# One layer of an RWKV-7/GLA backbone: the MLP's first product in seven block products for eight, and three passes over the tokens for two

## Chip, cores and metric

The kernel runs on one core of a Trainium2 chip. The time is device microseconds (us) of one execution of the whole program, from its first to its last instruction and what lies around them; the figure compared is the median of several runs.

## The reference, cut

One layer is computed for 256 prompt tokens and 2048 sample tokens, 2304 in all, with 1024 channels and an MLP width of 4096, in fp32. The change lies in the last four lines.

```python
def _block(x, mod, shift, states, p):
    sh1, sc1, gt1, sh2, sc2, gt2 = jnp.split(mod, N_MOD, axis=-1)
    h = _rmsnorm(x, p['norm1_g']) * (1.0 + sc1) + sh1
    o, new_states = _mixer(h, shift, ..., p)      # RWKV-7 and GLA heads, both directions
    x = x + gt1 * o
    h = _rmsnorm(x, p['norm2_g']) * (1.0 + sc2) + sh2
    f = jnp.square(jax.nn.relu(h @ p['mlp_w1'])) @ p['mlp_w2']
    x = x + gt2 * f
    return x, new_states                          # then y = _rmsnorm(x, final_norm_g)
```

The gate `gt2` (a row of 1024 numbers) is one for the prompt tokens and another for the sample tokens.

## The kernel before

Three stages follow each other: projections (`proj`), the two recurrences (`mixers`), and the `Tail`, which holds everything that is changed. The tail works on 18 units of 128 tokens. Their places in the token order are the list `UNITS`; units 9 and 10 are the prompt.

Numbers are kept at fp32 accuracy on TensorE (PE) by splitting each operand in two: `split` makes `hi`, a copy cast to fp32r on ScalarE (ACT), and `lo`, the rest, on VectorE (DVE). `mm3` then runs three matmuls (hi hi, hi lo, lo hi) into one bank of PSUM. There are 8 such banks.

- `unit(u)` normalises the mixers' outputs, multiplies by the output weights `wo` (48 matmuls of 512 columns), adds the residual, sends the result to DRAM (`d.x2`, "d_x" in the rows), norms again and transposes. The result, h2, is channels by tokens. Units 0 to 8 send it to DRAM (`d.h2`, "d_h" in the rows, 8 writes of 64 KB each). Units 9 to 17 split six of its eight row blocks straight into the SBUF tiles `h2h` and `h2l`; two row blocks go through DRAM, since their place is taken until then by `mh`, the split operand of the output product.
- `mlp(u0)` does 9 units, 1152 tokens, in 16 rounds. Round `gi` covers 256 of the 4096 middle channels. For each half of it a 512 KB piece of the first weights is loaded into `w1r` and split, and multiplied with three chunks of 384 tokens (8 x 3 matmuls of 384 columns each). Relu, square and split give `f`. Then each unit's second product (2 x 2 x 3 matmuls of 512 columns) is added to its accumulator `acc` by DVE. After round 13 (`PRE`) the accumulators are multiplied by the gate and the residual is added; in the last two rounds each product is multiplied by the gate as it is added. Round 15 ends with the final norm and the store.
- `reload` brings h2 back from DRAM between the two passes, `mlp(9)` and `mlp(0)`, 24 loads of 192 KB, each followed by a split.

All of the tail's instructions are recorded by `Plan`, which follows who reads and writes which part of a tile, gives each instruction an assumed cost, and issues them by list scheduling: of the instructions that could start, the one with the longest path behind it goes first. So the order on each engine isn't the order of the code. Every recorded instruction has line 534 in the profile, and the names of tiles tell them apart: "woh" and "wol" are the hi and lo parts of what lies over the output weights (first weights, second weights, f), "rr" is the buffer of relu and square. All DMAs are issued by SyncE (SP).

Of the kernel before, what the change touches and what calls it, by code (L numbers as in the profile page):

```python
# [185 lines left out]
BK_TAIL = [2, {"ps_t": 3, "ps_h": 1, "ps_m": 3, "ps_1": 3, "ps_2": 2}]  # L186
# [87 lines left out]
class Plan:  # L274
# [50 lines left out]
    def add(self, eng, method, args, kw):  # L325

        i = len(self.ops)
        if method == "matmul" and not kw["start"] and (args[1].dtype != F32R or len(self.ops[-1][1]) < 3):
            i -= 1
# [1211 lines left out]
MR = 2  # L1541
# [11 lines left out]
class Tail:  # L1553

    def __init__(self, g, es):
# [14 lines left out]
        self.rings = {
            "yo": acc[0:2], "gbs": [x[:, 0:1536] for x in acc[2:4]], "xt": [x[:, 1536:2048] for x in acc[2:4]],
            "x": [acc[4], xa, xb], "raw": [w1r, w2r, xa, xb], "m": halves(gf), "hf": halves(hf),
            "mh": [[w[:, 7 - i, 0:1024].rearrange("p (k n) -> p k n", k=8) for w in self.h] for i in range(MR)],
            "w1r": [w1r], "w2r": [w2r], "x2": [xa], "t": halves(xb), "r": [r[:, 0:384], r[:, 384:768]],
            "w1": [[wo[0][x][:, 1024 * i:1024 * i + 1024].rearrange("p (k n) -> p k n", k=8) for x in range(2)] for i in range(2)],
            "w2": [[wo[0][x][:, 2048 + 1024 * i:3072 + 1024 * i] for x in range(2)] for i in range(2)]
            + [[wo[1][x][:, 2304:3328] for x in range(2)]],
            "f": [[wo[1][x][:, 1152 * i:1152 * i + 1152] for x in range(2)] for i in range(2)],  # L1580
        }
        self.turn = dict.fromkeys(self.rings, 0)
        self.junk = r.bitcast(mybir.dt.bfloat16)[:, 0:1024]
# [30 lines left out]
    def unit(self, u):  # L1614
# [69 lines left out]
        for i in range(2):  # L1684
# [9 lines left out]
            k0 = 4 * i  # L1694
            k1 = k0 + 4 if u == 17 else min(k0 + 4, 8 - MR) if u >= 9 else k0
            if k1 > k0:
                cs = slice(128 * (u - 9), 128 * (u - 9) + 128)
                split(g, self.h[0][:, k0:k1, cs], self.h[1][:, k0:k1, cs], hf[:, 0:k1 - k0])
            for k in range(k1, k0 + 4):
                nc.sync.dma_start(out=d.h2[128 * k:128 * k + 128, us], in_=hf[:, k - k0])  # L1700

    def reload(self, k, u0, n):
        g = self.g
        raw = self.next("hf")[:, 0:128 * n]
        g.nc.sync.dma_start(out=raw, in_=g.d.h2[128 * k:128 * k + 128, 128 * u0:128 * (u0 + n)])
        cs = slice(128 * (u0 % 9), 128 * (u0 % 9 + n))
        split(g, self.h[0][:, k, cs], self.h[1][:, k, cs], raw)
# [133 lines left out]
```

## Time and profile before

| | us |
|---|---|
| median of 3 runs (lowest to highest) | 3704.69 (3702.34 to 3711.63) |
| the profiled execution | 3709.88 |
| its span, first to last instruction | 3708.2 |
| TensorE busy | 3504.4 (95%) |
| VectorE busy | 2249.8 (61%) |
| ScalarE busy | 1871.6 (50%) |
| GpSimd busy | 200.7 (5%) |

The projections and mixers fill the span up to about 1820 us, the units run to about 2090, the first MLP pass to about 2880 and the second to about 3690. Busy times are sums of single durations on one engine; engines work at the same time, so an engine's idle time costs something only where another waits for it. Matmuls overlap in PE's pipeline; the distance from one start to the next is the rate.

### The profile page before, as it was taken

What the parts mean: (1) busy time and instruction counts of PE and PEld (TensorE: products, weight loads), DVE (VectorE), ACT (ScalarE), POOL (GpSimd) and SP (SyncE); (2) the same over time, 40 slices, a digit from 0 to 9 for tenths busy, and PEclk for the clock granted to TensorE, in tenths of its full rate; (3) what the DMA queues carried; (4) which work ended last, traced back from release to release, by engine and by line L of the source; (5) the groups of instructions that cost most, each with busy time, mean ns of one, the idle gap of its engine ahead of it and who ended that gap; (6) DMA issues with size and microseconds to landing.
All of it is one profiled execution on the core that took longest, in us unless ns stands there. A gap on an engine that the chain in (4) does not pass through costs nothing.

```text
span 3708.2 us, 74382 instructions
## 1 busy us (share of the span) xinstructions
PE 3504.4 (95%) x28927; PEld 3104.1 (84%) x28927; DVE 2249.8 (61%) x4991; ACT 1871.6 (50%) x4264; POOL 200.7 (5%) x500
## 2 busy tenths in 40 slices
PE   6999999999999779999699999999999999999998
PEld 4989888977888668888587899999999899999997
DVE  2665778756888778788487534334447734444357
ACT  5566857775568567788567622222223422222222
POOL 1111002200011210100000000000000000000000
PEclk8999999999999889899799999999999999999999
DMA  5356335532245655565688411111114311111122
GB/s 170 110 152 172 103 84 167 145 107 56 62 129 160 181 159 168 154 193 164 168 250 248 146 40 46 35 40 46 46 43 136 130 34 46 46 46 40 46 70 101
DMA packets 504207, 411.47 MB, mean 111 GB/s; under 512 B 87761, under 2 KB 458926, under 8 KB 503854
## 3 DMA queue, kind: packets, MB, share of 16 engines
q1 hardware_dynamic: 503854, 406.71, 37.6%
q8 instruction: 228, 3.74, 0.4%
q14 instruction: 125, 1.02, 0.1%
HBM read 287.03 MB, written 119.55 MB: 110 GB/s over the span
## 4 chain that ended last, share of the span: by engine, by line
PE 46%; DMA 2%; DVE 1%; ACT 1%; issue 0%; DVEq 0%; SPq 0%; ACTq 0%
PE ps L534 46%; DVE acc L534 1%; DMA hf<-d_h 0%; ACT hf L534 0%; DMA xb<-in_w_out_dram 0%; DVE xb L534 0%; DMA xa<-in_x_sample_dram 0%; DVE h2l L534 0%; DMA d_h<-hf 0%; DMA xb<-in_x_sample_dram 0%; DMA acc<-in_x_prompt_dram 0%; DMA xa<-in_x_prompt_dram 0%; ACT xb L534 0%; ACT h2h L534 0%; DVE gf L534 0%
## 5 line engine op out<-in xcount | busy, mean ns | idle before, releaser
L534 DVE TENSOR_TENSOR acc<-acc,ps 128x512 f32<-128x512 f32 x468 | 319.8, 688 | 504.0 <-PE ps L534 503.5
L534 PE MATMUL ps<-hh,w_hi 128*128 128x384 f32 (+3 forms) x1736 | 594.2, 342 | 5.2 <-ACT w_hi L534 3.9
L534 PE MATMUL ps<-hh,w_lo 128*128 128x384 f32 (+3 forms) x1736 | 548.7, 316 | 0.9 <-DVE w_lo L534 0.9
L534 PE MATMUL ps<-hl,w_hi 128*128 128x384 f32 (+3 forms) x1736 | 549.0, 316 | 0.0
L534 ACT ACTIVATE rr<-ps 128x384 f32<-128x384 f32 x192 | 94.4, 492 | 869.2 <-PE ps L534 861.5
L534 PE MATMUL ps<-h2l,woh 128*128 128x384 f32 x1536 | 516.4, 336 | 0.6 <-DVE h2l L534 0.4
L534 PE MATMUL ps<-h2h,woh 128*128 128x384 f32 x1536 | 513.9, 335 | 0.9 <-ACT h2h L534 0.9
L534 PE MATMUL ps<-h2h,wol 128*128 128x384 f32 x1536 | 514.1, 335 | 0.0
L534 PE MATMUL ps<-woh,wol 128*128 128x512 f32 x1152 | 456.2, 396 | 0.0
L534 PE MATMUL ps<-wol,woh 128*128 128x512 f32 x1152 | 454.0, 394 | 0.0
L534 PEld LDWEIGHTS ps<-hh,w_hi 128*128 128x128 f32 (+1 forms) x1736 | 328.4, 189 | 39.1 <-issue 10.3
L534 PEld LDWEIGHTS ps<-hl,w_hi 128*128 128x128 f32 (+1 forms) x1736 | 329.0, 190 | 2.9 <-DVE hl L534 0.4
L534 PEld LDWEIGHTS ps<-hh,w_lo 128*128 128x128 f32 (+1 forms) x1736 | 327.9, 189 | 3.4 <-DVE w_lo L534 1.7
L534 PEld LDWEIGHTS ps<-h2l,woh 128*128 128x128 f32 x1536 | 288.3, 188 | 23.3 <-DVE h2l L534 1.6
L534 PEld LDWEIGHTS ps<-h2h,woh 128*128 128x128 f32 x1536 | 288.4, 188 | 21.2 <-ACT h2h L534 1.6
L534 PE MATMUL ps<-woh,woh 128*128 128x512 f32 x774 | 301.1, 389 | 0.5 <-ACT woh L534 0.5
L534 PEld LDWEIGHTS ps<-h2h,wol 128*128 128x128 f32 x1536 | 288.3, 188 | 0.0
L534 DVE TENSOR_TENSOR wol<-rr,woh 128x384 fp32r<-128x384 f32 x192 | 103.7, 554 | 267.4 <-ACT woh L534 267.4
L534 PEld LDWEIGHTS ps<-woh,wol 128*128 128x128 f32 x1152 | 215.9, 187 | 46.7 <-DVE wol L534 0.9
L534 PEld LDWEIGHTS ps<-wol,woh 128*128 128x128 f32 x1152 | 215.9, 187 | 31.2
L534 ACT CAST woh<-rr 128x384 fp32r<-128x384 f32 x192 | 95.7, 515 | 201.4 <-PE ps L534 198.4
L534 PEld LDWEIGHTS ps<-woh,woh 128*128 128x128 f32 x774 | 145.4, 188 | 21.5 <-ACT woh L534 0.8
(296 smaller groups left out, 6735.7 us busy)
## 6 DMA issues: line engine op xcount, KB each, us to landing
w_raw<-in_w_in_dram SPq DMA_DIRECT2D x72, 512.0 KB
w1r<-in_mlp_w_dram SPq DMA_DIRECT2D x64, 512.0 KB
w2r<-in_mlp_w_dram SPq DMA_DIRECT2D x64, 512.0 KB
BK<-d_bk SPq DMA_DIRECT2D x36, 512.0 KB
AR<-d_ar SPq DMA_DIRECT2D x72, 256.0 KB
acc<-d_yo SPq DMA_DIRECT2D x36, 512.0 KB
w_raw<-in_ada_w_dram SPq DMA_DIRECT2D x32, 512.0 KB
d_ar<-s SPq DMA_DIRECT2D x56, 256.0 KB
```

The costliest lines, as they stand in the source:

```text
L534: getattr(getattr(self.nc, eng), method)(*[at(x) for x in args], **{k: at(x) for k, x in kw.items()})
```

## The change

- A pass now takes 6 units, 768 tokens, so there are three: units 0 to 5, 12 to 17, and 6 to 11. The last one holds both prompt and sample units.
- In each round the first product is one product of 2 by 2 blocks, done as seven (`blocks`). The first weights' piece, now 1 MB for 256 channels, is cut in halves of channels and of the 1024 summed rows (a11, a12, a21, a22). Four sums of them are made by DVE in place. h2 is cut in halves of the summed rows and of the tokens. Seven blocks of it, four plain ones and three sums (t1, t2, t3; b21 less t2 for the sixth), are kept in `h2h` and `h2l`. Each part is 4 x 3 matmuls of 384 columns. The four results are made from the seven by seven additions of 384 columns on DVE and one copy on ACT (`u1`). Winograd's form of the sums is used.
- The seven blocks are made in `reload`, for which h2 goes to DRAM whole. A load is 128 rows by 384 tokens. Three of the seven `lo` parts and one sum are made on GpSimd (POOL). For the first pass the blocks 0 to 3 are made while the units run, and 4 to 6, which lie over half of the output weights, behind them from a second set of loads.
- In the two passes that have one gate (`one`), the second weights' rows are multiplied by the gate before they are split, and `acc` is loaded with the residual before the pass. The last pass keeps the old way.
- The final norm is a function of its own (`final`).

The core of the diff:

```diff
-        self.h = [tp.tile([128, 8, 1152], F32R, name=f"h2{x}") for x in "hl"]
+        self.h = [tp.tile([128, 7, 4, 384], F32R, name=f"h2{x}") for x in "hl"]
+        wf = [t(f"wf{x}", 6656, F32R) for x in "hl"]
+        wo = [[w[:, 0:4096] for w in wf], [w.rearrange("p s k n -> p (s k n)")[:, 6656:10752] for w in self.h]]
...
+            "w1r": [w1r], "w2r": [w2r], "x2": [xa], "t": halves(xb), "r": cut[0:4], "u": cut[4:8], "s1": [s1],
...
+    def reload(self, u0, first=False):
...
+        def both(k, i, x):
+            hi, lo = [y[:, i, k] for y in self.h]
+            nc.scalar.copy(hi, x)
+            eng = nc.gpsimd if i in (1, 5, 6) else nc.vector
+            eng.tensor_tensor(out=lo, in0=x, in1=hi.bitcast(F32), op=ALU.subtract)
+        for k in range(4):
+            b11, t3, b22, b21 = load(k, 0, 0), load(k, 0, 1), load(k, 1, 1), load(k, 1, 0)
+            t1 = self.next(b)
+            TT(out=t1, in0=t3, in1=b11, op=ALU.subtract)
+            both(k, 0, b11)
+            t2 = self.next(b)
+            TT(out=t2, in0=b22, in1=t1, op=ALU.subtract)
+            nc.gpsimd.tensor_tensor(out=t3, in0=b22, in1=t3, op=ALU.subtract)
+            both(k, 2, t2)
+            both(k, 1, b21)
+            both(k, 3, t3)
+            if not first:
+                TT(out=b21, in0=b21, in1=t2, op=ALU.subtract)
+                both(k, 4, t1)
+                both(k, 5, b21)
+                both(k, 6, b22)
...
+    def blocks(self, gi):
...
+        raw = self.next("w1r").rearrange("p (k n) -> p k n", k=8)
+        nc.sync.dma_start(out=raw, in_=w1[:, :, 256 * gi:256 * gi + 256])
+        a11, a12, a21, a22 = [raw[:, 4 * j:4 * j + 4, 128 * i:128 * i + 128] for i in range(2) for j in range(2)]
+        def part(w, b):
+            wh, wl = self.next("w1")
+            split(g, wh, wl, w)
+            ps = self.ps.tile([128, 512], F32, name="ps_1")[:, 0:384]
+            for k in range(4):
+                mm3(g, ps, wh[:, k], wl[:, k], self.h[0][:, b, k], self.h[1][:, b, k], k == 0, k == 3)
+            return ps
...
+        nc.scalar.copy(u1, part(a11, 0))
+        TT(out=s1, in0=a21, in1=a22, op=ALU.add)
+        TT(out=a21, in0=a11, in1=a21, op=ALU.subtract)
+        TT(out=a11, in0=s1, in1=a11, op=ALU.subtract)
+        u2 = add("u", u1, part(a11, 2))
+        out(0, 0, add("r", u1, part(a12, 1)))
+        u3 = add("u", u2, part(a21, 3))
+        p5 = part(s1, 4)
+        out(1, 1, add("r", u3, p5))
+        TT(out=u2, in0=u2, in1=p5, op=ALU.add)
+        TT(out=s1, in0=a12, in1=a11, op=ALU.subtract)
+        out(1, 0, add("r", u3, part(a22, 5)))
+        out(0, 1, add("r", u2, part(s1, 6)))
...
     def mlp(self, u0):
+        if one:
+            self.gate(grp[0], 1)
+            for i in turn:
+                residual(i, acc[i])
         for gi in range(16):
+            fs = self.blocks(gi)
...
                 nc.sync.dma_start(out=raw, in_=a["mlp_w2"][0, 128 * f:128 * f + 128, :])
+                if one:
+                    TT(out=raw, in0=raw, in1=self.gt, op=ALU.mult)
                 vh, vl = self.next("w2")
                 split(g, vh, vl, raw)
...
-        t.mlp(9)
-        for k in range(8):
-            for u0 in (0, 3, 6):
-                t.reload(k, u0, 3)
-        t.mlp(0)
+        for u0 in (0, 12, 6):
+            t.reload(u0, u0 == 0)
+            t.mlp(u0)
```

Where the planner puts it. On DVE, in the middle of a pass before, additions into `acc` stand almost alone, with a split of f or of a weight between them:

```order
L534 TENSOR_TENSOR wol_21711<-w1r,woh_21710 128x1024
L534 TENSOR_TENSOR wol_21713<-rr,woh_21712 128x384
L534 TENSOR_TENSOR acc_21717<-acc_21717,ps_21738 128x512
L534 TENSOR_TENSOR acc_21717<-acc_21717,ps_21739 128x512
L534 TENSOR_TENSOR acc_21717<-acc_21717,ps_21734 128x512
L534 TENSOR_TENSOR acc_21717<-acc_21717,ps_21733 128x512
L534 TENSOR_TENSOR acc_21718<-acc_21718,ps_21736 128x512
L534 TENSOR_TENSOR acc_21718<-acc_21718,ps_21737 128x512
```

On DVE in the middle of the first pass now ("wf" holds the split weights and f, "q" the sums u and r, "s" the sum s1):

```order
L534 TENSOR_TENSOR q<-q,ps_21730 128x384
L534 TENSOR_TENSOR w1r<-s_21714,w1r 128x4x128
L534 TENSOR_TENSOR w2r<-w2r,gt 128x1024
L534 TENSOR_TENSOR acc<-acc,ps_21731 128x512
L534 TENSOR_TENSOR acc<-acc,ps_21732 128x512
L534 TENSOR_TENSOR acc<-acc,ps_21734 128x512
L534 TENSOR_TENSOR wfl<-q,wfh 128x384 x2
L534 TENSOR_TENSOR wfl<-w1r,wfh 128x512 x3
L534 TENSOR_TENSOR wfl<-s_21714,wfh 128x512
L534 TENSOR_TENSOR s_21714<-w1r 128x512
```

Between the additions now stand gate products, weight sums, part sums and several splits; the order repeats every round.

On POOL, the queue's end before, with the last work of the mixers and none in the tail:

```order
L534 MEMSET X_13335 128x1024
L534 MEMSET X_13335 128x32
L534 COPY NB_13298<-NB_13298 32x32x32 x2
L534 MEMSET NB_13298 32x32x32 x2
L1834 UNCONDITIONAL_BRANCH
```

And the queue's end now, which is the second half of the last pass change:

```order
L534 TENSOR_TENSOR q<-q 128x384
L534 TENSOR_TENSOR h2l<-q,h2h 128x384
L534 TENSOR_TENSOR q<-xa,q 128x384
L534 TENSOR_TENSOR h2l<-q,h2h 128x384
L534 TENSOR_TENSOR h2l<-xa,h2h 128x384 x3
L534 TENSOR_TENSOR h2l<-q,h2h 128x384
L1919 UNCONDITIONAL_BRANCH
```

Behind the mixers POOL gets sums and `lo` parts of blocks of h2, 48 in all, 16 for each pass.

On SP at the first pass change now, stores of the old accumulators, loads of the residual into the same places, loads of h2 blocks and of weights stand mixed in one queue:

```order
L534 DMA out_y_s_dram<-acc 128x1024 x2
L534 DMA w2r<-in_mlp_w_dram 128x1024
L534 DMA acc<-d_x_92 128x1024 x2
L534 DMA xb<-d_h_93 128x384
L534 DMA out_y_s_dram<-acc 128x1024
L534 DMA w1r<-in_mlp_w_dram 128x8x256
L534 DMA acc<-d_x_92 128x1024
```

Before, the pass change had stores and h2 loads there, and no loads into `acc`:

```order
L534 DMA out_y_s_dram<-acc_21716 128x1024
L534 DMA hf<-d_h_93 128x384 x2
L534 DMA gt<-d_mod 128x1024
L534 DMA out_y_s_dram<-acc_21716 128x1024
L534 DMA hf<-d_h_93 128x384 x2
```

A residual load can start only when the store of the same accumulator has read it.

More of the change, by code (lines that the diff above doesn't have):

```diff
@@ L185 @@
 BK_MIX = [1, {"ps_z": 3, "ps_u": 4, "ps_y": 2, "ps_o": 2}]
-BK_TAIL = [2, {"ps_t": 3, "ps_h": 1, "ps_m": 3, "ps_1": 3, "ps_2": 2}]
+BK_TAIL = [2, {"ps_t": 3, "ps_h": 1, "ps_m": 3, "ps_1": 5, "ps_2": 3}]
 class View:
@@ L327, in add @@
         i = len(self.ops)
-        if method == "matmul" and not kw["start"] and (args[1].dtype != F32R or len(self.ops[-1][1]) < 3):
+        if method == "matmul" and not kw["start"] and self.ops[-1][0] == eng and (args[1].dtype != F32R or len(self.ops[-1][1]) < 3):
             i -= 1
@@ L1571, in __init__ @@
         halves = lambda x: [x[:, 0:512], x[:, 512:1024]]
+        cut = [q[:, 384 * i:384 * i + 384] for i in range(8)]
         self.rings = {
[L1573 to L1580, printed above, removed]
+            "yo": [acc[:, 0:2048], acc[:, 2048:4096]], "gbs": [w1r[:, 0:1536], acc[:, 4096:5632]],
+            "xt": [acc[:, 5632:6144]], "x": [xb, xa, w2r],
@@ L1693, in unit @@
                     scale=g.A2[:, k, grp:grp + 1])
[L1694 to L1702, printed above, removed]
-        g = self.g
[L1704 to L1707, printed above, removed]
+            for j in range(4):
+                k = 4 * i + j
+                nc.sync.dma_start(out=d.h2[128 * k:128 * k + 128, us], in_=hf[:, j])
@@ new lines, in reload, with load @@
+    def reload(self, u0, first=False):
+        g = self.g
+        nc, TT = g.nc, g.nc.vector.tensor_tensor
+        b = "b0" if first else "b"
+        def load(k, i, j):
+            r0, c0 = 128 * (4 * i + k), 128 * (u0 + 3 * j)
+            x = self.next(b)
+            nc.sync.dma_start(out=x, in_=g.d.h2[r0:r0 + 128, c0:c0 + 384])
+            return x
+        def both(k, i, x):
[19 more added lines that the diff above has]
+                both(k, 6, b22)
+        b = "b1"
+        for k in range(4) if first else ():
+            b11, t1, b22, t4 = load(k, 0, 0), load(k, 0, 1), load(k, 1, 1), load(k, 1, 0)
+            TT(out=t1, in0=t1, in1=b11, op=ALU.subtract)
+            both(k, 4, t1)
+            TT(out=t4, in0=t4, in1=b22, op=ALU.subtract)
+            both(k, 6, b22)
+            TT(out=t4, in0=t4, in1=t1, op=ALU.add)
+            both(k, 5, t4)
@@ L1726, in mlp @@
                 ws.append((vh, vl))
[L1727 to L1740 removed]
+            for i in turn:
+                if not one and gi > PRE and i in new:
+                    self.gate(grp[i], 1)
                 ts_ = slice(128 * i, 128 * i + 128)
[L1742 removed]
                 for c in range(2):
```

113 lines of the change are left out of this document (60 added, 53 removed).

## The prediction

> **What bounds the kernel now.** I read the page's head first, then a table by stage, then who TensorE (PE) waits for, then single instructions. The page's head and its costliest VectorE (DVE) row:
>
> ```profile
> span 3708.2 us, 74382 instructions
> PE 3504.4 (95%) x28927; PEld 3104.1 (84%) x28927; DVE 2249.8 (61%) x4991; ACT 1871.6 (50%) x4264; POOL 200.7 (5%) x500
> ...
> L534 DVE TENSOR_TENSOR acc<-acc,ps 128x512 f32<-128x512 f32 x468 | 319.8, 688 | 504.0 <-PE ps L534 503.5
> ```
>
> Busy time by stage (columns: stretch, its length, then PE, weight load, DVE, ACT, POOL busy with counts, granted PE clock, DMA share, GB/s). The units run to about 2090, then come the two MLP passes; their border lies in 2860 to 2930.
>
> ```profile
> 1820.00:2090.00 270.00, 244.79 (x1175) 200.49 (x1175) 200.32 (x426) 183.07 (x533) 0.00 (x0) 0.94 0.84 240
> 2090.00:2130.00 40.00, 37.12 (x191) 32.67 (x190) 18.84 (x29) 22.57 (x49) 0.00 (x0) 1.00 0.32 101
> 2130.00:2860.00 730.00, 730.00 (x3684) 661.83 (x3683) 318.88 (x445) 183.42 (x325) 0.00 (x0) 1.00 0.17 52
> 2860.00:2930.00 70.00, 69.61 (x345) 62.01 (x344) 63.38 (x118) 39.77 (x97) 0.00 (x0) 1.00 0.53 182
> 2930.00:3690.00 760.00, 760.00 (x3824) 687.85 (x3823) 342.23 (x490) 192.84 (x355) 0.00 (x0) 1.00 0.16 50
> 3690.00:3708.20 18.20, 1.58 (x7) 0.96 (x6) 13.45 (x29) 4.68 (x17) 0.00 (x0) 0.62 0.50 191
> ```
>
> In the MLP PE never rests, at clock 1.00, while DVE works 44% of the time (318.88 of 730) and the DMA engines 17%. All that PE waited for there after 2130:
>
> ```profile
> PE ps L534 <- ACT h2h L534: 0.2, 1, 0.2
> ```
>
> So the MLP is bound by the count of matmuls. A busy PE isn't yet the rate, since the 0.33 us of a matmul overlaps the next; the rate is the distance of the starts (timeline, start and duration):
>
> ```profile
> 2399.96 0.33 PE L534 MATMUL ps<-h2h,woh 128*128 128x384 f32 x1
> ...
> 2402.91 0.33 PE L534 MATMUL ps<-h2h,wol 128*128 128x384 f32 x1
> 2403.08 0.39 PE L534 MATMUL ps<-woh,woh 128*128 128x512 f32 x1
> ...
> 2404.24 0.40 PE L534 MATMUL ps<-woh,wol 128*128 128x512 f32 x1
> ```
>
> The same weight load, one round apart (the queue of SyncE, SP, in the timeline):
>
> ```profile
> 2211.40 0.37 SPq L534 DMA_DIRECT2D w1r<-in_mlp_w_dram  x1
> 2261.44 0.37 SPq L534 DMA_DIRECT2D w1r<-in_mlp_w_dram  x1
> ```
>
> Seventeen steps of 384 columns in 2.95 us are 173.5 ns each; five of 512 in 1.16 us are 232 ns. A round (one gi) has 2x3x8x3 = 144 of the first and 9x2x2x3 = 108 of the second: 24.98 + 25.06 = 50.04 us, and the weight load does return after 50.04 us.
>
> **PE: what is removed.** A round becomes 7 parts x 4 x 3 = 84 matmuls of 384 columns and 6x2x2x3 = 72 of 512: 14.57 + 16.70 = 31.28 us. There are 48 rounds for 32. The 512 total stays at 3456; the 384 total goes from 4608 to 4032. So 576 x 173.5 ns = **-99.9 us**, all on the path. The Trainium skill ("TensorE: Matmul & The Clock Gate", Part 1) gives a warm matmul N/2.4 GHz + 2.5 ns, 162.5 ns here, by which the gain would be 93.6 us. The rows are 11 ns slower at a granted clock of 1.00, so the measurement decides.
>
> **DVE: what is added per round.** Its prices (name, count | busy, mean ns):
>
> ```profile
> L534 DVE TENSOR_TENSOR wol<-rr,woh 128x384 fp32r<-128x384 f32 x66 | 35.7, 554 | 107.4 <-ACT woh L534 107.4
> L534 DVE TENSOR_TENSOR wol<-w2r,woh 128x1024 fp32r<-128x1024 f32 x22 | 26.9, 1223 | 4.7 <-ACT woh L534 4.7
> L534 DVE TENSOR_TENSOR h2l<-gf,h2h 128x512 fp32r<-128x512 f32 x36 | 24.6, 684 | 8.9 <-ACT h2h L534 8.7
> L534 DVE SCALAR_TENSOR_TENSOR acc<-acc,xr,gf 128x1024 f32<-128x1024 f32 x18 | 22.8, 1280 | 0.5 <-ACT xr L534 0.5
> ```
>
> A round now has 7 weight splits and 4 sums of weight blocks, each 512 wide (11 x 0.69 = 7.5); 7 sums of products and 4 splits of f, 384 wide (11 x 0.554 = 6.1); 2 gate products and 2 splits of w2, 1024 wide (4 x 1.22 = 4.9); 12 additions into acc (12 x 0.688 = 8.3). Together 26.8 us, 86% of 31.28 us, where it was 44%. The cover is the 4.5 us left over. The window 2860 to 2930 is the nearest row for such a load: DVE 63.38 of 70 us (91%), and PE lost 0.39 us. Bounds: 0, and 1 us a round if each chain through DVE slips once. Nearest to that row: **+3 us** in all. ACT (25% of the stage) loses a third of its activations a round and gains casts in the measure of DVE's splits; it stays far from full.
>
> **Pass changes, now two.** A change must rebuild 7 block sums in 4 row blocks: on DVE 7 x 4 = 28 operations of 384 columns (15.5 us), and the six norms that end a pass (6 x 1.28 and three small operations of some 0.15 each, 10.4 us). Over four rounds DVE has 4 x 26.8 + 25.9 = 133.1 us against PE's 125.1 at the first change: 8.0 too much. The last pass has no gate product on w2, so there it is 128.2: 3.1 too much. The old change held 24 splits and 9 norms, but its rounds were 50 us long.
>
> The residual now stands in acc from the start of the two passes with one gate: six loads of 512 KB, each on SP behind the store of the same acc, and the next w2 loads behind them. Stores, residuals, blocks and two rounds of weights are 3.1 + 3.1 + 3.1 + 4.2 MB; the window 2860 to 2930 moved 182 GB/s at a share of 0.53, so 13.5 MB need some 40 us of the 62 us of two rounds: hidden, and if not, within the bounds below.
>
> GpSimd (POOL) gets 16 of these operations in each change. Its price and what it does to DVE (its row among the groups, then three rows of the timeline):
>
> ```profile
> L534 POOL TENSOR_TENSOR s<-s 128x256 f32<-128x256 f32 x28 | 30.9, 1104 | 38.8 <-DVE s L534 32.6 <-PE ps L534 3.2 <-issue 2.9
> ```
>
> ```profile
> 267.27 0.42 DVE L534 TENSOR_TENSOR s<-s,Ep 128x256 f32<-128x256 f32 x1
> ...
> 267.44 0.84 POOL L534 TENSOR_TENSOR s<-s 128x256 f32<-128x256 f32 x1 [0.37 <-DVE s L534]
> 267.61 0.96 DVE L534 TENSOR_TENSOR s<-s 128x256 f32<-128x256 f32 x1
> ```
>
> The first DVE operation took 0.42 us alone; its like, begun while POOL ran, took 0.96 us and ended 0.29 us after POOL did. So the two don't work side by side here. At 384 columns a POOL operation is 0.84 x 1.5 = 1.26 us (1.66 by the group's mean), 16 of them 20 us. The Trainium skill says why ("SBUF — State Buffer", on the shared port pair): a GpSimd operation and a DVE operation with two SBUF inputs lock each other out for a whole instruction. This trace agrees (0.96 for 0.42 us), and the rule speaks against this change. No row here shows whether a DVE operation that reads PSUM waits too, and part of POOL's time falls where DVE is idle, so I take half, 10 us. About 5 us of lag can rest in PSUM banks (three product banks of six 232 ns matmuls are 4.2 us). So 8 + 10 - 5 = 13 and 3 + 10 - 5 = 8: **+21 us**; bounds 0, and 8 + 20 + 3 + 20 = 51 without the lag.
>
> **The units and the start.** All 18 units now send all of h2 to DRAM: 144 writes for 88, 56 x 64 KB = 3.7 MB, and 16 loads of 192 KB of the first block sums stand among them: 6.8 MB, 27 us at the 256 GB/s of the next row. Every write also passes SP's queue.
>
> ```profile
> 1860.00:2000.00 140.00, 139.41 (x688) 115.36 (x687) 111.55 (x244) 93.65 (x295) 0.00 (x0) 1.00 0.91 256
> 2000.00:2020.00 20.00, 15.72 (x74) 12.40 (x73) 14.33 (x29) 14.62 (x42) 0.00 (x0) 0.91 0.96 273
> ```
>
> In the first of these the first nine units, which already send all eight pieces, keep PE at 139.41 of 140 us beside a DMA share of 0.91; the later ones will look like them, less 18 splits on ACT and DVE. Bounds 0 and +27; I take **+4**, near the first row.
>
> Then the first pass begins. Before, 2.9 us were lost in 2090 to 2130. Now blocks 4 to 6 lie over half of the output weights and can be written only after the last unit's products: 8 POOL operations, 10.1 us by the above, against five parts of 2.08 us (10.4 us) that can run meanwhile; half of the loads wait for the buffers of the other half, and a load is not quick:
>
> ```profile
> 2457.23 0.34 SPq L534 DMA_DIRECT2D w2r<-in_mlp_w_dram  x1
> ...
> 2461.59 1.06 ACT L534 CAST woh<-w2r 128x1024 fp32r<-128x1024 f32 x1 [0.66 <-DMA w2r<-in_mlp_w_dram]
> ```
>
> 512 KB took 4.4 us. Bounds -2.9 and +12; I take **+6**.
>
> **The end.** The last pass holds both gates: 12 products and additions of 1024 in round 13 (14.6 us), 24 gate products in the last two rounds (16.5 us) and the norms (10.4 us), over four rounds 139 us of DVE on 125.1 of PE: 14 too much. Most of such a backlog already lies behind the last matmul (DVE 13.45 of the last 18.2 us). Bounds 0 and +14; **+4**.
>
> **Sum.** -99.9 + 3 + 21 + 4 + 6 + 4 = -61.9: span 3646.3. The profiled execution took 3709.9 us, 1.7 outside its span, so 3648.0; it was 5.2 above the median of the runs shown (3704.7), so I predict **3643 us**.
>
> **Rivals.**
> - *All of it is covered.* The 91% row speaks for it; DVE's demand of over 100% at the changes against it. Losses of 10 to 20 us: 3615 to 3625, say 3620. Chance 0.12.
> - *Each round slips.* DVE is in order, at 86%, and its sums wait for PE while PE waits for its splits. At 0.5 to 1 us in 48 rounds, 24 to 48 us for the 3 taken: 3664 to 3688, say 3680. The only row at such a load is 70 us long. Chance 0.15.
> - *POOL blocks DVE for all of its time, with no lag to absorb it:* 51 us for 21, and as much again at the start and the end, some 10: 3683. The 0.96 us row is for it; that DVE also reads PSUM is against it. Chance 0.08.
> - *Slower: the single buffer of the first weights.* A round's 1 MB load now starts only when the sixth part's weights are split, and the next round's first sums wait for it. In DVE's queue 13 operations stand between (8.0 us by the prices above), and 4.5 us are idle. The load takes between 4.4 us (the row) and twice that. At over 8.0 + 4.5 us every round waits; with 62/48 = 1.3 us more, at 13.8 us, the gain is gone. A load of 14 us would cost 48 x 1.5 = 72 us: 3715. Chance 0.07.
> - *That it doesn't remove the matmuls:* no; the built program has 6960 rows of 384 columns for 7536, and 4320 of 512 in both.
>
> **How the numbers follow.** The forecast, with losses between 20 and 60 us, 3625 to 3665, has 0.58. The range 3613 to 3693 runs from 10 us of losses to the upper ends of the second and third rivals, and leaves out the last rival and some 0.06 of tails. A difference under 0.3% (11 us) can't be told from none: faster is below 3693.6. The forecast, the covered case and nearly all of the second and third rivals lie there: 0.88. Within 0.3% the ends of those two, 0.05; slower the last rival, 0.07.
>
> **What would show it.** In the first and second pass, one w1r load every 31.3 us, DVE 86% busy, PE without idle time; POOL bursts at two places with DVE operations of about 0.55 us stretched towards 1.5 us, and PE idle there by 13 and 8 us; PE idle under 10 us at the start; a tail like the old one. A period over 31.8 us, or idle PE put down to w1r's load, would make the prediction wrong; so would a distance of starts other than 173 and 232 ns.

## Result and profile after

The changed kernel takes 3674.6 us (median of 4 runs, 3669.7 to 3677.9) against 3703.9 us (4 runs, 3702.3 to 3711.6): a ratio of 0.9916, 95% interval 0.9898 to 0.9934. It is faster by 29 us, inside the range and 32 us above the number predicted. The profiled executions differ by 35.5 us of span, 3672.7 against 3708.2. The page's head and the costliest VectorE row after:

```profile
span 3672.7 us, 74476 instructions
PE 3427.1 (93%) x28351; PEld 3014.3 (82%) x28351; DVE 2730.7 (74%) x5859; ACT 2071.7 (56%) x4652; POOL 258.9 (7%) x548
...
L534 DVE TENSOR_TENSOR acc<-acc,ps 128x512 f32<-128x512 f32 x540 | 352.0, 683 | 47.9 <-PE ps L534 46.3
```

The 576 matmuls are gone (28927 to 28351), and DVE has 481 us more to do. By stage (columns as before: stretch, length, then PE, weight load, DVE, ACT, POOL busy with counts, clock, DMA share, GB/s): the units, the start of the MLP, then steady rounds and pass changes in turn, and the end.

```profile
1820.00:2096.00 276.00, 243.97 (x1132) 197.41 (x1133) 201.82 (x426) 178.00 (x524) 11.86 (x10) 0.92 0.89 254
2096.00:2145.00 49.00, 37.60 (x162) 30.52 (x161) 35.88 (x55) 28.63 (x62) 7.80 (x6) 0.83 0.57 180
2145.00:2570.00 425.00, 425.00 (x2127) 382.84 (x2126) 325.84 (x515) 163.78 (x301) 0.00 (x0) 1.00 0.22 69
2570.00:2690.00 120.00, 107.65 (x506) 92.75 (x505) 106.38 (x176) 59.63 (x128) 19.35 (x16) 0.97 0.42 139
2690.00:3080.00 390.00, 389.55 (x1947) 350.61 (x1946) 303.19 (x478) 152.35 (x277) 0.00 (x0) 1.00 0.22 68
3080.00:3200.00 120.00, 110.40 (x532) 97.94 (x532) 103.50 (x171) 61.14 (x130) 20.37 (x16) 0.96 0.34 111
3200.00:3560.00 360.00, 360.00 (x1790) 323.73 (x1789) 261.06 (x416) 142.71 (x254) 0.00 (x0) 1.00 0.22 68
3560.00:3673.00 113.00, 96.20 (x459) 83.78 (x457) 99.02 (x162) 41.45 (x88) 0.00 (x0) 0.95 0.32 111
```

In the steady rounds PE is busy for the whole stretch although DVE works 77% of it. The load of the first weights comes back every 31.27 us, (2435.65 - 2310.56) / 4, where 31.28 was predicted:

```profile
2310.56 0.38 SPq L534 DMA_DIRECT2D w1r<-in_mlp_w_dram  x1
...
2435.65 0.38 SPq L534 DMA_DIRECT2D w1r<-in_mlp_w_dram  x1
```

So the time is lost elsewhere. A count shows how much: 120 us of full rate hold 120 x 156 / 31.28 = 598 matmuls. The two pass changes hold 506 and 532, so they lack 92 and 66, or 18 and 13 us. Below, the *loss* of a stretch is its length less 0.1735 us for each 384-column and 0.2315 us for each 512-column matmul that starts in it; for the two stretches of 120 us that gives 18.3 and 14.5 us. The tables take some 155 us around each change, so that all of its loss falls inside: 18.6 and 14.3 us. *Units* is the time from the mixers' last row of matmuls to the last product of the units; it is good to about 0.7 us. Loss in the MLP is split into the start (the first 45 us), change 1, change 2 and the end. The whole difference of the two spans, in this measure:

| part | before | after | difference | predicted |
|---|---|---|---|---|
| mixers' end (not changed) | 1806.2 | 1799.8 | -6.4 | 0 |
| matmuls removed | | | -99.9 | -99.9 |
| units | 276.0 | 295.6 | +19.6 | +4 |
| start | 7.5 | 22.3 | +14.8 | +6 |
| pass changes | 0.5 | 18.6 + 14.3 | +32.4 | +21 |
| steady rounds | 1.8 | 2.8 | +1 | +3 |
| end and what follows the last matmul | 16.4 | 19.4 | +3 | +4 |

They sum to -35.5. The losses aren't all idle time. PE is idle for 12.4 and 9.6 us of the two changes (120 less 107.65 and 110.40). The rest, some 6 and 5 us, is in matmuls that don't come at full rate. The last one before a pause counts with its whole 0.39 us, since nothing overlaps it. And behind the longest pause of change 2 the granted clock is 0.50 for a while, and matmuls of 512 columns start 0.43 us apart, where they started 0.22 us apart before it:

```profile
3131.83 0.39 PE L534 MATMUL ps<-wfl,wfh 128*128 128x512 f32 x1
3132.05 0.39 PE L534 MATMUL ps<-wfh,wfl 128*128 128x512 f32 x1
3137.83 0.76 PE L534 MATMUL ps<-wfh 128*128 128x512 f32 x1 [5.39 <-DVE acc L534]
3138.39 0.63 PE L534 MATMUL ps<-wfl,wfh 128*128 128x512 f32 x1
3138.82 0.63 PE L534 MATMUL ps<-wfh,wfl 128*128 128x512 f32 x1
```

```profile
3135.00:3141.00 6.00, 3.17 (x8) 2.53 (x9) 6.00 (x9) 3.08 (x8) 2.91 (x3) 0.50 0.58 184
```

Summed over the matmuls of the trace, 3.0 us of change 1, 3.7 us of change 2 and 5.8 us of the start are lost where the granted clock is 0.50.

The mixers' 6.4 us is scatter: that code is the same in every run here, and its end lay between 1787.7 and 1806.2 us. Experiments whose effect is smaller than this are therefore read by stage rather than by total time.

### The profile page after: what moved, and what is told of

The parts are those of the page before. It is cut to its first block, busy times and chain, and to the rows that moved or that the text cites. A ratio compares the mean times of both kernels' runs of the same rounds, so it can differ in the third digit from the quotient of the medians.

```text
span 3672.7 us, 74476 instructions
## 1 busy us (share of the span) xinstructions
PE 3427.1 (93%) x28351; PEld 3014.3 (82%) x28351; DVE 2730.7 (74%) x5859; ACT 2071.7 (56%) x4652; POOL 258.9 (7%) x548
## 5 line engine op out<-in xcount | busy, mean ns | idle before, releaser
L534 PE MATMUL ps<-hh,w_hi 128*128 128x384 f32 (+3 forms) x1736 | 591.8, 341 | 4.0 <-ACT w_hi L534 2.9
L534 PE MATMUL ps<-wfh 128*128 128x512 f32 x1296 | 516.1, 398 | 34.2 <-ACT wfh L534 20.4
L534 PE MATMUL ps<-hh,w_lo 128*128 128x384 f32 (+3 forms) x1736 | 546.7, 315 | 1.2 <-DVE w_lo L534 1.2
L534 PE MATMUL ps<-hl,w_hi 128*128 128x384 f32 (+3 forms) x1736 | 546.9, 315 | 0.2 <-DVE hl L534 0.2
L534 PE MATMUL ps<-wfh,wfl 128*128 128x512 f32 x1296 | 517.0, 399 | 5.6 <-DVE wfl L534 5.6
L534 PE MATMUL ps<-h2l,wfh 128*128 128x384 f32 (+1 forms) x1488 | 511.5, 344 | 9.1 <-DVE h2l L534 8.7
L534 PE MATMUL ps<-h2h,wfh 128*128 128x384 f32 (+1 forms) x1488 | 513.2, 345 | 3.1 <-ACT wfh L534 1.8
L534 PE MATMUL ps<-h2h,wfl 128*128 128x384 f32 (+1 forms) x1488 | 512.1, 344 | 1.2 <-DVE wfl L534 1.1
L534 PE MATMUL ps<-wfl,wfh 128*128 128x512 f32 x1296 | 513.1, 396 | 0.0
L534 DVE TENSOR_TENSOR acc<-acc,ps 128x512 f32<-128x512 f32 x540 | 352.0, 683 | 47.9 <-PE ps L534 46.3
L534 PEld LDWEIGHTS ps<-hh,w_hi 128*128 128x128 f32 (+1 forms) x1736 | 326.6, 188 | 37.5 <-issue 10.3
L534 PEld LDWEIGHTS ps<-hl,w_hi 128*128 128x128 f32 (+1 forms) x1736 | 327.3, 189 | 3.0 <-DVE hl L534 0.6
L534 PEld LDWEIGHTS ps<-hh,w_lo 128*128 128x128 f32 (+1 forms) x1736 | 326.2, 188 | 3.7 <-DVE w_lo L534 2.0
L534 PEld LDWEIGHTS ps<-wfh 128*128 128x128 f32 x1296 | 246.7, 190 | 79.7 <-ACT wfh L534 23.4
L534 DVE TENSOR_TENSOR q<-q,ps 128x384 f32<-128x384 f32 x336 | 182.5, 549 | 171.9 <-PE ps L534 167.7
L534 PEld LDWEIGHTS ps<-h2l,wfh 128*128 128x128 f32 x1488 | 281.9, 189 | 30.0 <-DVE h2l L534 11.8
L534 PEld LDWEIGHTS ps<-wfh,wfl 128*128 128x128 f32 x1296 | 246.0, 190 | 68.3 <-DVE wfl L534 14.4
L534 PEld LDWEIGHTS ps<-h2h,wfh 128*128 128x128 f32 x1488 | 282.0, 190 | 22.7 <-ACT wfh L534 2.9
L534 ACT CAST wfh<-w1r 128x512 fp32r<-128x512 f32 x240 | 146.0, 618 | 272.9 <-PE ps L534 183.4
L534 PEld LDWEIGHTS ps<-h2h,wfl 128*128 128x128 f32 x1488 | 281.6, 189 | 9.1 <-DVE wfl L534 2.7
L534 PEld LDWEIGHTS ps<-wfl,wfh 128*128 128x128 f32 x1296 | 246.6, 190 | 42.5
L534 ACT ACTIVATE q<-q 128x384 f32<-128x384 f32 x384 | 197.8, 523 | 67.0 <-DVE q L534 58.0
```

What stands on the lines that cost most here:

```text
L534: getattr(getattr(self.nc, eng), method)(*[at(x) for x in args], **{k: at(x) for k, x in kw.items()})
```

## Experiments

Each starts from the changed kernel, the last versions from e_pre where it is said. The table gives medians, ratios to the kernel before with their intervals, and the stages of the profiled execution, all in us.

| run | median | ratio | units | start | change 1 | change 2 |
|---|---|---|---|---|---|---|
| changed kernel | 3674.6 | 0.9916 [0.9898, 0.9934] | 295.6 | 22.3 | 18.6 | 14.3 |
| e_merge | 3670.3 | 0.9911 [0.9895, 0.9927] | 295.7 | 16.5 | 17.8 | 14.3 |
| e_late | 3674.6 | 0.9926 [0.9908, 0.9943] | 278.9 | 39.0 | 20.2 | 16.1 |
| e_dum | 3686.6 | 0.9949 [0.9932, 0.9966] | 287.1 | 38.9 | 20.3 | 16.5 |
| e_dve | 3664.2 | 0.9892 [0.9874, 0.9910] | 296.5 | 23.2 | 16.4 | 12.8 |
| e_nonorm | 3667.6 | 0.9901 [0.9882, 0.9921] | 296.3 | 23.7 | 10.1 | 14.5 |
| e_two | 3685.3 | 0.9949 [0.9934, 0.9964] | 296.0 | 23.5 | 24.5 | 20.1 |
| e_unfold | 3691.6 | 0.9966 [0.9951, 0.9982] | 293.2 | 21.5 | 29.9 | 26.9 |
| e_md | 3660.1 | 0.9883 [0.9863, 0.9902] | 298.9 | 14.9 | 17.1 | 14.3 |
| e_pre | 3650.2 | 0.9864 [0.9849, 0.9878] | 294.0 | 13.4 | 16.6 | 1.4 |
| e_prext | 3660.6 | 0.9888 [0.9871, 0.9904] | 292.6 | 21.9 | 15.5 | 2.3 |
| e_res | 3669.9 | 0.9912 [0.9891, 0.9933] | 299.1 | 22.3 | 18.0 | 15.4 |
| e_preres | 3654.7 | 0.9867 [0.9848, 0.9886] | 296.3 | 13.4 | 16.0 | 2.3 |

### What the units lost: three runs

**e_merge**, fewer and larger writes of h2:

```diff
-    d.h2 = dram.tile([D, T], F32, name="d_h2")
+    d.h2 = dram.tile([128, KD * T], F32, name="d_h2")
...
-            for j in range(4):
-                k = 4 * i + j
-                nc.sync.dma_start(out=d.h2[128 * k:128 * k + 128, us], in_=hf[:, j])
+            nc.sync.dma_start(out=d.h2.rearrange("p (k t) -> p k t", k=KD)[:, 4 * i:4 * i + 4, us], in_=hf)
```

> Changed: the four 64 KB writes of h2 that end each half of a unit become one write of 256 KB (144 writes become 36; the same bytes). In the changed kernel the units took 295.6 us from the end of the mixers to their last product, before the change 276.1. Theory (the number of writes, each of which takes a turn in SyncE's queue while ScalarE waits for the buffer that it empties): the units fall to 275-284 us, the time from 3675 to 3655-3664 us. Rival 1 (bandwidth: the same bytes at a DMA share of 0.9): units 290-298, time 3670-3680. Rival 2 (the early block sums, which add work to VectorE and ScalarE among the units): the same as rival 1.

The theory fell: the units took 295.7 us. Only the start gained, 5.8 us. What the trace shows there is the queue of SyncE (SP): in the changed kernel, writes of the last units stand ahead of and among the loads for the second half of the block sums, and ScalarE waited 7 us for a buffer that such a write empties. Three rows of SP's timeline and one of ScalarE's, after:

```profile
2099.42 4.58 SPq L534 DMA_DIRECT2D d_h<-q  x8
...
2109.99 1.39 SPq L534 DMA_DIRECT2D d_h<-q  x3
...
2119.10 2.59 SPq L534 DMA_DIRECT2D d_h<-q  x3
```

```profile
2127.17 0.81 ACT L534 ACTIVATE q<-ps,modT,A 128x128 f32<-128x128 f32 x2 [6.99 <-DMA d_h<-q]
```

The Trainium skill ("SBUF — State Buffer", on the DMA setup-cost knee) advises larger transfers, since each pays a fixed 2 us or so. Among the units, where many transfers are under way at once and the DMA share is near 0.9, four times fewer writes changed nothing. The gain at the start goes the page's way, but the rows show turns in SP's queue there, and no run parts these from a fixed cost of each transfer.

**e_late** builds the first pass's sums after the units, as the other passes do: `t.reload(u0)` for `t.reload(u0, u0 == 0)`.

> Changed: the first pass makes its block sums as the other two do, after the units; none of the 16 early loads and early sums stands among the units any more. Theory (the h2 writes cost the units their 19.6 us): units 289-296 us, and the start of the MLP loses 10-20 us more, time 3683-3700 us. Rival (the early loads and sums cost it): units 275-282 us, the start loses the same 10-20 us more, time 3664-3680 us.

The rival held: the units fell to 278.9 us, 2.9 above the kernel before. So the 56 added writes, with the 18 splits that went away and the smaller buffers, cost 3 us, and the early block sums with their loads the other 16.7. But the start then lost 16.7 us more: units and start together take 317.9 us either way. Building early bought nothing. The same 220 us of the units, of the kernel before, of the changed kernel and of this run:

```profile
1850.00:2070.00 220.00, 212.11 (x1026) 174.15 (x1026) 168.32 (x363) 147.23 (x444) 0.00 (x0) 0.98 0.82 234
```

```profile
1850.00:2070.00 220.00, 200.07 (x944) 163.17 (x943) 168.58 (x360) 145.74 (x437) 9.82 (x8) 0.95 0.89 250
```

```profile
1850.00:2070.00 220.00, 212.62 (x1033) 175.51 (x1032) 158.70 (x343) 148.43 (x442) 1.10 (x1) 0.98 0.90 259
```

In the last PE does as many matmuls as before the change (1033 and 1026), at a DMA share of 0.90 for 0.82.

**e_dum** is the same with the 16 early loads left in, into buffers that nothing reads:

```diff
+        if u0 == 0:
+            for k in range(4):
+                for i, j in ((0, 0), (0, 1), (1, 1), (1, 0)):
+                    r0, c0 = 128 * (4 * i + k), 128 * 3 * j
+                    nc.sync.dma_start(out=self.next("b0"), in_=g.d.h2[r0:r0 + 128, c0:c0 + 384])
```

> Changed: block sums of the first pass late, as in the run with late sums (units 278.9 us, start 39.0 us), but with the 16 early loads of h2 (3.1 MB) left among the units, into buffers that nobody reads. Theory (the units lack DMA bandwidth: their DMA share is 0.83 to 1.00): units 289-296 us, time 3682-3695 us. Rival (the early sums on VectorE, ScalarE and GpSimd cost the units their time, not the loads): units 277-282 us, time 3670-3680 us.

Neither: 287.1 us, just between. The loads alone cost 8.2 us; the remaining 8.5 us come only when the sums read what was loaded. In this run 220 us hold 987 matmuls:

```profile
1850.00:2070.00 220.00, 204.78 (x987) 166.05 (x986) 157.87 (x344) 142.71 (x431) 1.02 (x1) 0.98 0.91 260
```

The loads are 3.1 MB, 12 us at 260 GB/s, so two thirds of their time could not be hidden at this DMA share.

Where the other 8.5 us arise is not shown. The sums stand in the queues of DVE, ScalarE and POOL, but the loads differ as well. In e_dum SP has issued the 16 early ones by 1995 us, in the changed kernel by 2032 us, and there eight of the second set follow among the units, where e_dum has three of its later loads. Issuing some of them holds SP for about 4 us, where 0.4 us is usual, and all transfers behind wait. After, two or three loads in each row:

```profile
2010.55 4.88 SPq L534 DMA_DIRECT2D q<-d_h  x2
...
2027.02 4.74 SPq L534 DMA_DIRECT2D q<-d_h  x3
...
2044.71 4.62 SPq L534 DMA_DIRECT2D q<-d_h  x2
```

In e_dum one such issue took 4.08 us. No run parts the loads and SP's queue from the engines' work.

### GpSimd beside VectorE

**e_dve** gives all of POOL's sums and splits to DVE:

```diff
-            eng = nc.gpsimd if i in (1, 5, 6) else nc.vector
+            eng = nc.vector
...
-            nc.gpsimd.tensor_tensor(out=t3, in0=b22, in1=t3, op=ALU.subtract)
+            TT(out=t3, in0=b22, in1=t3, op=ALU.subtract)
```

> Changed: all block sums and splits that GpSimd did in the MLP are VectorE's; GpSimd does nothing there. VectorE gets 16 operations of some 0.55 us (8.8 us) more in each pass change. Theory (GpSimd and VectorE shut each other out, so that a GpSimd operation costs VectorE 0.5 to 0.9 us of the 1.0 to 1.3 us that it lasts): the changes lose 18 and 14 us as now, within 4 us each, time 3667-3682 us. Rival (the sharing pays): the changes lose 27 and 23 us, the start some 4 us more, time 3690-3700 us. Rival (GpSimd blocks VectorE for all of its time): the changes lose 10 and 6 us, time 3655-3662 us.

By stage the theory held: without POOL the changes lost 16.4 and 12.8 us, 2.2 and 1.5 us less than with it. The time, 3664.2 us, is below the theory's 3667 to 3682, but 7 of the 8.4 us between the spans of the two profiled executions are the mixers' end, which the edit does not touch. In the changed kernel the operations of the two engines alternate where both read two operands from SBUF. POOL's rows, then DVE's:

```profile
2607.37 1.27 POOL L534 TENSOR_TENSOR xa<-xb,xa 128x384 f32<-128x384 f32 x1 [0.96 <-DVE q L534]
2608.60 1.34 POOL L534 TENSOR_TENSOR q<-q 128x384 f32<-128x384 f32 x1
2611.44 2.16 POOL L534 TENSOR_TENSOR h2l<-q,h2h 128x384 fp32r<-128x384 f32 x2 [1.51 <-ACT h2h L534]
```

```profile
2607.21 0.55 DVE L534 TENSOR_TENSOR q<-q 128x384 f32<-128x384 f32 x1
2607.68 1.37 DVE L534 TENSOR_TENSOR q<-xb,q 128x384 f32<-128x384 f32 x1
2608.97 1.37 DVE L534 TENSOR_TENSOR xa<-q 128x384 f32<-128x384 f32 x1
...
2611.68 1.87 DVE L534 TENSOR_TENSOR acc<-acc,ps 128x512 f32<-128x512 f32 x3
```

The operation that began before POOL's took 0.55 us, the next two 1.37 us each. The three additions that read PSUM (acc<-acc,ps) lie wholly beside POOL's operations and take 1.87 us, as three do elsewhere. This answers what the prediction had left open: a DVE operation with an operand in PSUM does not wait for POOL. The Trainium skill ("SBUF — State Buffer", who interferes with whom) says both, that two SBUF inputs contend with GpSimd's reads and one does not; the trace agrees. The changed kernel and this run, change 1:

```profile
2570.00:2690.00 120.00, 107.65 (x506) 92.75 (x505) 106.38 (x176) 59.63 (x128) 19.35 (x16) 0.97 0.42 139
```

```profile
2570.00:2690.00 120.00, 109.42 (x515) 95.42 (x514) 110.47 (x198) 61.18 (x132) 0.00 (x0) 0.97 0.41 135
```

DVE did 22 more operations in only 4.1 us more. At 0.55 us each they are 12.1 us, so POOL's presence had cost DVE up to 8 us here. Counted by the rows it is less at change 1 and more at change 2: 7 and 12 operations of 384 columns are stretched beyond 0.7 us, by 5.3 and 9.1 us in all, around the 10 taken in the prediction. Sixteen operations on POOL save DVE 8.8 us and cost it about as much.

### What fills a pass change

**e_nonorm** leaves out `final`'s norm in the first two passes.

```diff
+        if u0 == 6:
             ss = self.sm.tile([128, 2], F32, name="ss")
...
```

> Left out: the final norm of the first two passes, whose rows are stored unnormalised (12 of 18 row blocks). It takes 6 x 1.28 us and 18 small operations, some 10 us, from VectorE at each pass change, and two activations per row block from ScalarE. Theory (VectorE's work bounds the changes): they lose 8 and 4 us instead of 18 and 14, time 3652-3658 us. Rival (the loads of h2 and the residuals in SyncE's queue bound them): the changes lose 16-18 and 12-14 us, time 3670-3678 us.

Change 1 lost 8.5 us less; change 2 lost as much as before. The theory, a balance of all DVE work around a change, holds for the first and not for the second. The second seen closer, 30 us of the changed kernel and of this run:

```profile
3125.00:3155.00 30.00, 21.07 (x79) 16.70 (x78) 28.93 (x40) 17.58 (x40) 16.33 (x13) 0.83 0.28 84
```

```profile
3080.00:3200.00 120.00, 110.78 (x533) 98.50 (x532) 96.96 (x149) 55.42 (x104) 20.58 (x16) 0.96 0.34 111
3125.00:3155.00 30.00, 21.24 (x80) 17.26 (x79) 29.91 (x40) 14.14 (x29) 15.89 (x13) 0.83 0.38 122
```

Over 120 us DVE has 23 us to spare without the norms, and still PE does 80 matmuls in those 30 us where full rate is 150. PE's longest wait here is the one of 5.39 us shown above, for a PSUM bank that DVE's additions into acc had not emptied. DVE is full in this burst: it holds the block sums and splits, while the norms of change 2 come after it in DVE's order. At change 1 five of the six stand inside it.

**e_two** makes the sums of all passes in two steps, as the first pass does: `t.reload(u0, True)`.

> Changed: the second and third pass make their block sums in the two steps of the first pass: blocks 0 to 3 from 16 loads of h2, then blocks 4 to 6 from 16 more loads, with 8 VectorE operations more per change. Theory (a change is short of VectorE because its 28 sums and splits can only stand between the last use of a block and the first use of the new one, not because of the demand over four rounds): blocks 0 to 3 are free earlier than 4 to 6, so the work is spread over the last six us of the parts too; the changes lose 10-14 and 7-11 us instead of 18.6 and 14.3, time 3664-3670 us. Rival (VectorE's total work bounds them): 8 x 0.55 us more in each, 20-24 and 16-20 us, time 3680-3688 us.

The rival's numbers came: 24.5 and 20.1 us. My idea that an earlier start of blocks 0 to 3 would spread the work fell. 4.4 us more of DVE work cost 5.9 and 5.8 us. The run doubles the loads of h2 too, and where PE lost most DVE was not quite full and the DMA share was high:

```profile
2620.00:2640.00 20.00, 11.50 (x35) 7.38 (x34) 17.25 (x31) 10.31 (x25) 6.53 (x5) 0.63 0.90 308
```

So part of it may be the loads'.

**e_unfold** undoes the other half of the change, `one = False`: the gate is applied to the sums in the last three rounds of every pass, and nothing begins with the residual.

> Undone: the folding of the gate into the second weights and the sums that begin with the residual, in all three passes (the last pass has neither anyway). VectorE loses 2 x 1.22 us a round in 32 rounds and gains 6 gate products and 6 additions of 1024 columns (14.6 us) in round 13 and 24 gate products of 512 (16.5 us) in rounds 14 and 15, before each change. Theory (the folding takes this work from the place where VectorE is short): the changes lose 6-15 us more each, as the last pass loses 6.5 us at its end where it has this work; time 3685-3705 us. Rival (the loss arises in the last half round only, where the block sums stand): the changes lose 18 and 14 us as now, within 4 us, time 3668-3680 us.

The theory held: 29.9 and 26.9 us, 11.3 and 12.6 more. The folding is worth 17 us of the total (3691.6 against 3674.6) and 24 us by the two changes; what it does there is to take DVE work away. The gate products on w2 that it adds to the steady rounds cost nothing: between the start and change 1 both kernels lose 0.6 us.

### Versions made from this

**e_md** joins e_merge and e_dve.

> Changed: two edits together, the h2 writes of half a unit in one DMA and GpSimd's block sums on VectorE. Alone the first took 5.8 us from the start, the second 2.2 and 1.5 us from the changes. If they add up: units 294-298 us, start 15-18 us, changes 15-17 and 12-14 us, span less the mixers' part 1863-1869 us, time 3656-3666 us. If the merged writes helped only because GpSimd was in VectorE's way at the start: start 20-24 us, time 3664-3672 us.

By the medians the gains add up: 4.3 and 10.4 us alone, 14.5 us together. By stage they do so at the start (14.9 us) only: the changes lost 17.1 and 14.3 us, so at change 2 nothing of e_dve's 1.5 us is left. A difference of that size at a change is not to be relied on.

**e_pre** also takes the subtractions out of the changes. They are made in the early rounds of the pass before and kept in DRAM:

```diff
+            TT(out=t1, in0=t3, in1=t1, op=ALU.subtract)
+            TT(out=t3, in0=t2, in1=t3, op=ALU.subtract)
+            TT(out=t2, in0=t2, in1=t1, op=ALU.subtract)
+            TT(out=t4, in0=t4, in1=t2, op=ALU.subtract)
+            for n, y in enumerate((t2, t3, t1, t4)):
+                nc.sync.dma_start(out=self.summed(u0, n, k), in_=y)
...
+        for i in (0, 2, 1, 3, 4, 5, 6):
+            for k in range(4):
...
+                nc.sync.dma_start(out=x, in_=src)
+                hi, lo = [y[:, i, k] for y in self.h]
+                nc.scalar.copy(hi, x)
+                nc.vector.tensor_tensor(out=lo, in0=x, in1=hi.bitcast(F32), op=ALU.subtract)
```

> A version made from the findings: merged h2 writes, no GpSimd operations in the MLP (both as in the run with the two edits together, where the changes lost 17.1 and 14.3 us), and the 16 subtractions that make a later pass's block sums moved into the early rounds of the pass before: results go through DRAM (16 loads and 16 stores of 192 KB more per change, and 28 loads instead of 16 at the change itself). VectorE has 16 x 0.55 = 8.8 us less at each change. Theory (a change costs what VectorE has too much in it, as 4.4 us more cost 5.9): the changes lose 7-11 and 4-8 us, the early rounds no more than 3 us, time 3640-3652 us. Rival (the splits and loads that stay in the change are as long a chain without the subtractions): changes 14-18 and 12-15 us, time 3656-3668 us. Rival (2.3 MB more of loads at the change): changes 18-25 us.

This is the fastest kernel: 3650.2 us, ratio 0.9864 [0.9849, 0.9878], below the changed kernel's interval. Change 2 vanished, 1.4 us, and the same 30 us hold 149 matmuls for 79 (L535 is the helper that was L534, one line lower in this file):

```profile
3125.00:3155.00 30.00, 29.75 (x149) 26.59 (x148) 28.45 (x55) 18.18 (x45) 0.00 (x0) 1.00 0.45 156
```

Change 1 kept 16.6 us, as the first rival has it; at change 2 the theory's side came, and by more than it said.

What made change 2 vanish isn't parted. Its loss fell by 12.9 us, the work taken out of DVE is 8.8 us, and in these 30 us DVE is as full as before (28.45 us for 28.93). So a full DVE alone does not stop PE. The edit also changes the order: `reload2` finishes one block after the other, where `reload` makes all seven blocks of a row block at once. Its splits are spread from 3079 to 3130 us between the other operations of DVE, while in the changed kernel 23 of 28 stand between 3129 and 3153 us. A version with the new order and the subtractions left in place was not run.

**e_prext** adds a second slot for the units' product buffer, `"xt": [acc[:, 5632:6144], w1r[:, 1536:2048]]`.

> The version with the subtractions made beforehand, and the units' product buffer (xt) given back its second slot, which it had before the change. Theory (the single slot makes VectorE's two operations per product wait for each other): units 5-10 us shorter than in the version without it. Rival (DMA bandwidth and the early sums set the units' time): units within 3 us of it.

The rival: units 292.6 us, within 1.4 us. The start was 8.5 us worse (21.9 us) and the run slower. The trace shows a cause: the second slot lies in `w1r`, so the first weights can't be loaded there until the last unit has used it. Their load, in e_pre and then in this run:

```profile
2062.31 0.38 SPq L535 DMA_DIRECT2D w1r<-in_mlp_w_dram  x1
```

```profile
2099.26 0.87 SPq L535 DMA_DIRECT2D w1r<-in_mlp_w_dram  x1
```

The last product of the units starts at 2087.1 us in e_pre and at 2094.4 us here; the MLP's first matmul follows 1.0 us later there, and 15.9 us later here.

**e_res** and **e_preres**, the second made from e_pre, test whether the norms matter at change 1 by their place. The second pass copies its first product into acc and adds the residual in round 8, so that the norms of the first pass need not come before the residual loads:

```diff
-            for i in turn:
-                residual(i, acc[i])
+            if u0 == 0:
+                for i in turn:
+                    residual(i, acc[i])
...
-                    if gi == 0 and not one:
+                    if gi == 0 and u0 != 0:
...
+            if gi == 8 and one and u0 != 0:
+                for i in turn:
+                    x = self.next("x2")
+                    residual(i, x)
+                    TT(out=acc[i], in0=acc[i], in1=x, op=ALU.add)
```

> Changed in the second pass alone: its sums in acc begin with a copy of the first product again, and the residual is added in round 8 (6 additions of 1024 columns, 7.3 us on VectorE among steady rounds); the gate stays folded. The norms that end the first pass then need not be done before the residual's loads. Theory (at the first change the norms of the pass before stand ahead of the block sums, because the next pass's residual loads wait for them; without the norms this change lost 10.1 instead of 18.6 us): first change 10-14 us, second 13-16, steady rounds as now, time 3666-3671 us. Rival (the norms' work counts, not their place): first change 17-20 us, time 3673-3679 us.

> The version with merged writes, no GpSimd and subtractions made beforehand (3650.2 us; first change 16.6, second 1.4 us), with the second pass's residual added in round 8 as well. Theory (the norms ahead of the splits are what is left at the first change): first change 3-9 us, time 3637-3644 us. Rival (the norms' work counts, not their place): first change 15-18 us, time 3648-3653 us.

The rival's numbers came twice: 18.0 and 16.0 us. But the edit moved little. Of the 28 splits of the change, counted over DVE and POOL, 22 already stood ahead of the first norm in the changed kernel, and 26 do in e_res; in e_pre it was 16, in e_preres 23. So the norms did not stand ahead of the block sums in the first place, and that only their work counts is not shown beyond e_nonorm's 8.5 us. The second run's loss is in three pieces:

```profile
2590.00:2610.00 20.00, 17.56 (x75) 14.52 (x74) 14.42 (x25) 13.03 (x31) 0.00 (x0) 0.91 0.60 188
2610.00:2660.00 50.00, 45.21 (x212) 39.06 (x212) 49.27 (x95) 26.05 (x61) 0.00 (x0) 0.97 0.46 158
2660.00:2740.00 80.00, 77.10 (x383) 67.95 (x381) 63.69 (x105) 29.80 (x54) 0.00 (x0) 1.00 0.47 150
```

By the same measure of loss they are 4.5, 7.8 and 4.3 us. In the second DVE is full (49.27 of 50). In the first it is not, and waits:

```profile
2595.94 0.69 DVE L535 TENSOR_TENSOR s<-w1r 128x512 f32<-128x512 f32 x1 [3.43 <-DMA w1r<-in_mlp_w_dram]
```

The load of the first weights has one buffer and stands in SP's queue among the 28 loads of the change, so this is a new wait. The third piece is where the third pass's subtractions begin. How much each would give back alone was not run, so for change 1 this stays open.

## Why the prediction was right, and where its sum was off

- **The number: inside the range by luck.** Of the sum's terms only the matmuls, the steady rounds and the end came out within 2 us. The time lies outside the forecast's own band, 3625 to 3665 us, by 10 us. The range holds it only because it was drawn wider for two rivals, rounds that slip and a POOL that blocks DVE for all of its time, and neither happened.
- **Matmuls, -99.9: right.** The round is 31.27 us. That a busy DVE (77% in steady rounds) makes each round slip was the second rival: 2.8 us in all steady rounds refute it. The single weight buffer, the rival on the other side, cost nothing there either. Its wait shows at the changes alone, on ScalarE more than on PE (waits after, 2560 to 2720: in total, times, longest):

```profile
ACT wfh L534 <- DMA w1r<-in_mlp_w_dram: 12.2, 4, 5.3
```

- **Steady rounds, +3 predicted, +1 measured.** DVE works 24.0 us in a round (325.84 x 31.27 / 425) and not 26.8, so the cover was larger than reckoned. The prediction added up durations, and operations that follow each other start closer than that: 0.47 us apart for 0.55 us in the rows of e_dve's section. For the 38 operations of a round, 0.08 us each is an estimated 3 us.
- **Pass changes, +21 predicted, +32.4 measured.** The step that failed is that the loss was taken as PE's idle time alone. PE idles for 12.4 and 9.6 us, close to the 13 and 8 foreseen; the sum had no term for the matmuls that come slower around each pause, some 6 and 5 us. Even so the idle time came out near by chance, since the balance over four rounds is not the mechanism. It says 2.7 us for change 2 without norms, even without the lag, where 14.5 us were lost and 9.2 of them idle, and 8 us for change 1 of e_pre, where 16.6 were lost and 11.1 idle. At change 2 the work stands in a burst of some 30 us that DVE fills, and PE's longest wait is for a PSUM bank. Whether a lag of 5 us is there at all, no run shows. POOL's cost was about right (5.3 and 9.1 us of stretched operations for 10), and the rival that it blocks DVE for all its time fell.
- **Units, +4 predicted, +19.6 measured.** The writes were sized well: 2.9 us by e_late, net of the splits that went away. The term named the early loads but took them and the sums as nearly covered. The loads cost 8.2 us by e_dum, and another 8.5 us come with the sums; whether on the engines, which the prediction took as relieved by 18 splits, or in SP's queue stays open. The upper bound, 27, held.
- **Start, +6 predicted, +14.8 measured**, above the bound of 12. The term reckoned the GpSimd operations and the loads' time, but not that the last units' writes still stand in SP's queue ahead of those loads, 5.8 us by e_merge, nor the matmuls at a granted clock of 0.50, which lose 5.8 us in this stretch and nothing in the same stretch before.
- **End, +4: +3 measured.** The last pass loses 6.5 us before its last matmul and 3.8 less behind it than the kernel before.

The three errors that count, 16, 9 and 11 us, are all on one side: work was put down to a cover that other work already used, and pauses of PE were counted at their own length only.

## To carry to other kernels

When matmuls are removed from a kernel in which TensorE is the bound, look for the places where the helpers' work can't be spread: a balance over rounds says little about a burst that has to fit between the last use of a buffer and the first use of its next contents. Moving such work earlier pays if it lands where there is slack (subtractions into steady rounds, together with a new order of the blocks: change 2 from 14.3 to 1.4 us) and not if it lands in another full stage (sums among the units: 16.7 us there for 16.7 us here). Giving GpSimd a share of VectorE's operations on SBUF operands gained nothing here: 16 operations of 0.55 us were bought with 5 to 9 us of waiting at each change. And a pause of TensorE is to be counted at more than its length: a third of what the changes lost here was not idle time.

## What the hardware showed that I had not expected

- After a pause of 5.39 us the granted clock was 0.50 and matmuls of 512 columns started 0.43 us apart, for 0.22 before the pause. Of 32.9 us lost in the two changes PE was idle for 22.0.
- Issuing a DMA from SP, usually some 0.4 us, took about 4 us for some loads among the units, at a DMA share near 0.9.
- A DVE operation with an operand in PSUM ran at its own speed beside POOL (three 128x512 additions in 1.87 us), while those with both operands in SBUF went from 0.55 to 1.37 us.
- At a DMA share near 0.9, the number of transfers did not matter (144 or 36 writes: 295.6 and 295.7 us), while 3.1 MB of loads cost 8.2 us.
